# Encoder layer on one core: a planner that counts a transfer's packets, bias copies made in the prompt's attention, and two more buffers for reloaded rows

## The chip, the core and the metric

The kernel runs on one core of one Trainium2 chip. Its engines are TensorE (PE, the matmuls; PEld is its weight load), VectorE (DVE), ScalarE (ACT), GpSimd (POOL) and SyncE (SP), and here SP issues nearly all transfers of the 16 DMA engines. The metric is the device time of one execution in microseconds (us). Before the change it is 1153.21 us, the median of 3 runs (1151.79 to 1153.78).

## The reference

One layer of a bidirectional encoder is applied with the same weights to two inputs: a prompt of 512 tokens and a sample of 1024 tokens, each 1024 wide, all in float32.

```python
h = rmsnorm(x, norm_g)
proj = h @ w_in
qa, ka, va, za, qb, kb, vb, zb, ga, gb = jnp.split(proj, np.cumsum(SPLITS)[:-1], axis=-1)
qa = rmsnorm(qa.reshape(B, L, H_A, HEAD_DIM), qn_a)     # ka, qb, kb likewise
oa = neighbourhood_attention(qa, ka, va, rpb_a) * jax.nn.silu(za)
oa = oa @ w_o_a
ob = window_gqa_attention(qb, kb, vb, t5_table, sink_b) * jax.nn.silu(zb)
ob = ob @ w_o_b
merged = jax.nn.sigmoid(ga) * oa + jax.nn.sigmoid(gb) * ob
return x + merged @ w_out
```

Branch A has 8 heads of 64 that attend to a clamped window of 8 by 16 neighbours on a grid 64 wide, with a learned relative bias `rpb`. Branch B has 8 query heads on 2 key heads, a window of 128 tokens to each side, a T5 bias and a sink logit.

## The kernel before

**Products.** A float32 product is made of three matmuls: each operand is split into a high part (ACT, a copy to a shorter mantissa) and a low part (DVE or POOL, the difference), and high*high, low*high and high*low are added up in PSUM. In the rows this is a group of three: `x<-hh,whi`, `x<-hl,whi`, `x<-hh,wlo` on lines 1292, 1293 and 1294 (512 columns each), and `p<-whi,hh`, `p<-wlo,hh`, `p<-whi,hl` on line 762 (384 columns).

**Stages.** The work runs in four stages: the prompt's attention (to about 213 us), the prompt's dense phase (to about 412 us; beside it the sample's rows are normalised), the sample's attention (to about 780 us) and the sample's dense phase. In an attention stage PE makes the projections of q, k, v (L762), transposes the normalised q and k (L862, from the tile `qk`), makes scores (L934), transposes the exponentials `sb` (L1001, after ACT's exp on L980) and multiplies with v (L1038). The norm of q and k before L862 is a chain over three engines: ACT squares the projection (`sq`, L781), DVE sums (`ss`, L786), POOL turns the sum into a factor (`rs_v` L793, `rs_r` L800), and DVE multiplies (`qk`, L817). In a dense stage come the gate paths z, the products with w_o_a and w_o_b, the merge gates g, and the output product with w_out.

**Fill products.** Some dense products need only `hh` and `hl`, the normalised rows, and are made inside the attention stages to fill PE's gaps: `d<-hh,fh` and its two partners. Each result leaves PSUM through one tile `fc` with a single buffer (L1523) and is stored to DRAM as `g_d` or `p_d` (L1408). The next leave can write `fc` only when the store before has landed.

**Bias copies.** Branch A's bias is read by each head as long rows. `expand` (L413) copies the table in DRAM into `rpb_x`, 16 copies of 96 KB for the prompt and 16 for the sample; in the attention stage a bias tile is loaded from there (L683). The prompt's copies are made at the start, and the sample's copies from 211.72 us on, in the prompt's dense phase.

**u loads.** In the sample's dense phase the gated branch outputs u are kept in DRAM (`u_d`) and loaded again for the last products (L1577) through the two buffers of the tile `ot`; they are split into high and low parts as tiles `T`.

**Normalising the sample.** For the sample's norm factors eight tiles of the input are loaded in the prompt's attention (L458, `xt<-in_x_s_dram`), and ACT squares and sums them (L461, tile `junk`).

**The order.** All instructions are put in order ahead of time by a list planner, the class `Flow`. Each operation has a priority, a planned duration on each engine that may take it, its operands and its tiles. `Flow.run` keeps a clock: whenever an engine is free it takes, by priority, the operation whose inputs have arrived and whose tiles have a free buffer. A transfer costs SP an issue time, its bytes queue behind the transfers before (`dma_free`), and it counts as landed some time after. What comes out is one fixed sequence for each engine. On the chip each engine works through its sequence in order and waits by semaphores; a late input then holds up everything behind it on that engine. So a change of any planned cost can move instructions anywhere.

```python
return self.op((("sp", 470),), lambda e: emit(), prio, lag=nbytes / 360, **kw)
...
    dma_free = max(dma_free, now + ns + 650) + got.lag
    at(dma_free + 950, 2, got)
```

## Time and profile before

| what | value |
|---|---|
| median of 3 runs | 1153.21 us (1151.79 to 1153.78) |
| the profiled execution's own time | 1154.72 us |
| its span in the profile | 1152.9 us |
| PE busy | 1133.5 us, 6127 matmuls |
| DVE, ACT, POOL busy | 829.1, 640.8, 258.9 us |
| DMA | 174.65 MB, 151 GB/s over the span |
| TensorE clock granted, mean | 0.998 |

The profile is of one execution. Times in its rows run from the start of the span. A matmul's busy time is modelled; what counts for PE is the distance from one start to the next, which is 0.227 us for 512 columns and 0.173 us for 384 columns where nothing is late. In a row of a timeline the bracket tells how long the engine stood idle before it, and what ended that.

### The profile page before, as it was taken

Reading aid. Unit: us, or ns where it says so; the run is one execution under the profiler, and the core shown is the slowest. Engines: PE = TensorE matmul, PEld = TensorE weight load, DVE = VectorE, ACT = ScalarE, POOL = GpSimd, SP = SyncE. Lnnn points to the kernel's source line nnn. Section 1 sums busy time; section 2 is a strip of 40 time slices with the busy share of each in tenths; the row PEclk is TensorE's granted clock in tenths of the full one; section 3 lists DMA queues with packets and bytes.
Section 4 is the critical chain, followed back from the end, with each engine's and each line's share of the span. In section 5 each row is a group of like instructions: output and inputs, shape, how many; then the busy total and the mean of one; then the engine's idle time right before and its main releaser. Section 6 shows DMA issues by size and latency. Waiting matters only on the chain.

```text
span 1152.9 us, 18448 instructions
## 1 busy us (share of the span) xinstructions
PE 1133.5 (98%) x6127; PEld 981.4 (85%) x6127; DVE 829.1 (72%) x1831; ACT 640.8 (56%) x1468; POOL 258.9 (22%) x316
## 2 busy tenths in 40 slices
PE   8999999999998999999999999999999999999998
PEld 6989998888876899999999898887888888788887
DVE  6777787387775467676768788866787875497984
ACT  6767887534343246565668988775432444342320
POOL 4642422000010033333322122110122231032110
PEclk9999999999999999999999999999999999999999
DMA  7844534587786432121213223238777756564062
GB/s 270 284 138 119 187 105 126 158 246 240 242 277 196 151 124 65 28 83 26 65 38 103 61 47 102 56 102 263 254 191 200 240 188 186 204 228 128 28 219 92
DMA packets 141313, 174.65 MB, mean 151 GB/s; under 512 B 38569, under 2 KB 77937, under 8 KB 141218
## 3 DMA queue, kind: packets, MB, share of 16 engines
q1 hardware_dynamic: 141218, 173.48, 49.5%
q8 instruction: 48, 0.79, 0.3%
q14 instruction: 47, 0.39, 0.1%
HBM read 134.51 MB, written 43.63 MB: 155 GB/s over the span
## 4 chain that ended last, share of the span: by engine, by line
PE 84%; DMA 6%; DVE 4%; ACT 2%; POOL 1%; issue 1%; SPq 1%; ACTq 0%; DVEq 0%; POOLq 0%
PE p L762 23%; PE x L1294 8%; PE x L1293 8%; PE x L1292 8%; PE x L1001 5%; PE x L1038 5%; PE x L934 4%; PE d L1292 4%; PE d L1294 3%; PE d L1293 3%; PE p L1293 3%; PE p L1292 3%; PE p L1294 3%; PE x L862 2%; DMA t_d<-xt 1%
## 5 line engine op out<-in xcount | busy, mean ns | idle before, releaser
L762 PE MATMUL p<-whi,hh 128*128 128x384 f32 x384 | 133.1, 347 | 0.0
L762 PE MATMUL p<-whi,hl 128*128 128x384 f32 x384 | 131.9, 344 | 0.0
L762 PE MATMUL p<-wlo,hh 128*128 128x384 f32 x384 | 130.9, 341 | 0.0
L1012 DVE TENSOR_TENSOR pp<-x,pp 128x512 fp32r<-128x512 f32 (+1 forms) x136 | 82.8, 639 | 46.2 <-ACT pp L1007 45.8
L980 ACT ACTIVATE sb<-sb,mx 128x384 f32<-128x384 f32 (+1 forms) x192 | 107.4, 564 | 15.4 <-DVE mx L971 15.1
L762 PE MATMUL p<-whi,hb 128*128 128x384 f32 x384 | 106.7, 345 | 0.0
L1174 ACT ACTIVATE whi<-raw 128x512 fp32r<-128x512 f32 (+1 forms) x124 | 73.7, 606 | 55.8 <-PE x L1293 23.0
L1294 PE MATMUL x<-T,wlo 128*128 128x512 f32 x256 | 99.9, 390 | 0.3 <-DVE wlo L1179 0.2
L1293 PE MATMUL x<-T,whi 128*128 128x512 f32 x256 | 99.9, 390 | 0.2 <-DVE T L1179 0.2
L1292 PE MATMUL x<-T,whi 128*128 128x512 f32 x256 | 99.7, 390 | 0.0
L1292 PE MATMUL x<-hh,whi 128*128 128x512 f32 (+1 forms) x232 | 90.5, 390 | 3.0 <-ACT hh L1174 2.9
L1293 PE MATMUL x<-hl,whi 128*128 128x512 f32 (+1 forms) x232 | 90.8, 391 | 0.5 <-DVE hl L1179 0.5
L1294 PE MATMUL x<-hh,wlo 128*128 128x512 f32 (+1 forms) x232 | 90.5, 390 | 0.2 <-DVE wlo L1179 0.2
L800 POOL TENSOR_TENSOR rs_r<-rs_v,mhalf 128x4 f32<-128x4 f32 (+1 forms) x72 | 85.6, 1189 | 5.5
L1179 DVE TENSOR_TENSOR wlo<-raw,whi 128x512 fp32r<-128x512 f32 (+1 forms) x101 | 67.3, 676 | 26.0 <-ACT whi L1174 23.8
L793 POOL TENSOR_SCALAR rs_v<-ss 128x4 f32<-128x4 f32 (+1 forms) x72 | 22.2, 308 | 282.9 <-DVE ss L786 270.0
L1007 ACT ACTIVATE pp<-x 128x512 fp32r<-128x512 f32 (+1 forms) x136 | 70.8, 560 | 17.5 <-PE x L1001 16.6
L1038 PE MATMUL x<-pp,v 128*128 128x256 f32 (+1 forms) x368 | 77.3, 321 | 0.0
L1179 POOL TENSOR_TENSOR wlo<-raw,whi 128x512 fp32r<-128x512 f32 (+1 forms) x23 | 29.9, 1300 | 202.8 <-DMA raw<-in_w_g_dram 119.8
L762 PEld LDWEIGHTS p<-whi,hh 128*128 128x128 f32 x384 | 72.5, 189 | 1.3 <-issue 1.0
L762 PEld LDWEIGHTS p<-wlo,hh 128*128 128x128 f32 x384 | 72.6, 189 | 1.0 <-issue 0.7
L762 PEld LDWEIGHTS p<-whi,hl 128*128 128x128 f32 x384 | 72.5, 189 | 0.8 <-issue 0.5
(354 smaller groups left out, 2917.2 us busy)
## 6 DMA issues: line engine op xcount, KB each, us to landing
raw<-in_w_g_dram SPq DMA_DIRECT2D x84, 256.0 KB
w<-in_w_att_dram SPq DMA_DIRECT2D x46, 384.0 KB
ot<-o_d SPq DMA_DIRECT2D x36, 256.0 KB
g_d<-C SPq DMA_DIRECT2D x34, 256.0 KB
raw<-in_w_z_dram SPq DMA_DIRECT2D x32, 256.0 KB
raw<-in_w_out_dram SPq DMA_DIRECT2D x32, 256.0 KB
fr<-in_w_g_dram SPq DMA_DIRECT2D x28, 256.0 KB
C<-g_d SPq DMA_DIRECT2D x24, 256.0 KB
```

The lines of the kernel that those rows point to most:

```text
L762: pe.matmul(ps.t[:, :GW], part[u](k), mv.t[:, c], start=k == 0 and m == 0, stop=k == KC - 1 and m == 2,)
L800: lambda e: nc.gpsimd.tensor_tensor(r.t[:, :nn], rv.t[:, :nn], mhalf[:, :nn], op=ALU.pow),
L980: act.activation(sb.t[:, :width], sb.t[:, :width], AF.Exp, bias=mx.t[:, col(i)], scale=-1.0, accum_out=sm.t[:, col(i)],)
L1001: pe.transpose(pt.t[:, u * P : (u + 1) * P], sbs[i].t[:, c * P : (c + 1) * P], ident)
L1007: lambda e, pt=pt, pp=pp, nn=nn: act.activation(pp.t[:, 0, :nn], pt.t[:, :nn], AF.Copy),
L1012: lambda e, pt=pt, pp=pp, nn=nn: dve.tensor_tensor(pp.t[:, 1, :nn], pt.t[:, :nn], pp.t[:, 0, :nn].bitcast(F32), op=ALU.subtract),
L1038: pe.matmul(out(), v.t[:, vs], mv(), start=first, stop=last)
L1174: (("act", ACT_(n)),), lambda e: act.activation(hi(), src(), AF.Copy), prio,
L1179: lambda e: engines[e].tensor_tensor(lo(), src(), hi().bitcast(F32), op=ALU.subtract), prio,
L1292: pe.matmul(out, hi.t[:, cs], mh(), start=first and k == 0, stop=False, **more)
L1293: pe.matmul(out, hi.t[:, cs], ml(), start=False, stop=False, **more)
L1294: pe.matmul(out, lo.t[:, cs], mh(), start=False, stop=last and k == len(ws) - 1, **more)
```

## The change

Four things are edited. First, the planner's model of a transfer. Its time in the DMA queue was the bytes by 360 a nanosecond; now it is the number of packets (`nbytes / run`) times a cost of each packet (`9 + run / 26` ns), over 16 engines. The landing is counted 1050 ns behind the queue instead of 950. The time of issue on SP was 470 ns for all; now it is 430 ns by default and 470, 560, 570, 610, 640 or 690 ns for some kinds. For the common load of 256 KB with packets of 2048 bytes the planned time from the start of the issue to the landing goes from 2.80 to 2.83 us; for the load of 512 KB with packets of 512 bytes (L556) from 3.53 to 4.15 us; for one bias copy from 2.62 to 2.94 us.

Second, the 16 bias copies of the sample are planned in the prompt's attention, with priorities 9 to 16 and a start tied to that stage's progress (`f.begun`); before, they came with the dense phase's priorities 54 to 61, behind the last exponential.

Third, the second half of the u loads (`n` = 1) uses the two buffers of the tile `fr`, which the first half does not use, so that four loads can be under way.

Fourth, the planned duration of one kind of multiply (`gv`, with a strided operand) is 890 instead of that of 512 columns.

```diff
-    def dma(self, emit, nbytes, prio, **kw):
-        return self.op((("sp", 470),), lambda e: emit(), prio, lag=nbytes / 360, **kw)
+    def dma(self, emit, nbytes, prio, run=2048, issue=430, **kw):
+
+        lag = nbytes / run * (9 + run / 26) / 16
+        return self.op((("sp", issue),), lambda e: emit(), prio, lag=lag, **kw)
...
                         dma_free = max(dma_free, now + ns + 650) + got.lag
-                        at(dma_free + 950, 2, got)
+                        at(dma_free + 1050, 2, got)
...
-        f.dma(lambda: nc.sync.dma_start(xt.t, x[t * P : (t + 1) * P, :]), 524288, load_prio, new=[xt], after=load_after)
+        f.dma(lambda: nc.sync.dma_start(xt.t, x[t * P : (t + 1) * P, :]), 524288, load_prio, 4096, 470, new=[xt], after=load_after)
...
-                f.dma(lambda h=h, lo=lo: expand(geo, h, lo), 196608, prios[h], after=after[h // 2]) for lo in range(2)
+                f.dma(lambda h=h, lo=lo: expand(geo, h, lo), 196608, prios[h], 1536, 690, after=after[h // 2]) for lo in range(2)
...
-                tt(gv, gv, lambda: ov().rearrange("p (i n) -> p n i", n=m), ALU.mult, n, prio, use=[sg, ot], into=[sg])
+                tt(gv, gv, lambda: ov().rearrange("p (i n) -> p n i", n=m), ALU.mult, 890, prio, use=[sg, ot], into=[sg])
...
-                    st = tile_("ot", n_ot)
+                    st = f.value(wpool, [P, nh], F32, "fr", 2) if n else tile_("ot", n_ot)
...
+    expand_ops(gs, [9 + h for h in range(8)], [[f.begun[NT_P, 9 + 2 * i]] for i in range(4)])
...
-    expand_ops(gs, [4 + h for h in range(8)], [[exps]] * 4)
```

The other lines of the diff hand packet sizes and issue times to `dma`. Lines of the changed kernel behind L190 are two further down (L413 is L415, L1292 is L1294).

What the planner makes of it: PE's sequence is the same, product for product, from about 213 to 412 us and from about 802 us to the end, but for the products around 980 to 1009 us. It differs in both attention stages, up to about 802 us. DVE, ACT and SP have the same sequences from about 340 to 410 us and from about 1030 us on.

Place one is SP in the prompt's attention, at about 84 to 92 us of the profile before (`o_d` is a store of attention output, `line_d` a bias load of branch B, `in_w_att` a weight load, `in_x_s` a tile for the sample's norm). Before:

```order
L1062 DMA o_d_81<-ot__1254 64x2x128
L1066 DMA o_d_81<-ot__1265 64x2x64 x2
L601 DMA w_1337<-in_w_att_dram 128x768
L601 DMA w_1347<-in_w_att_dram 128x768
L458 DMA xt<-in_x_s_dram 128x1024
L601 DMA w_1435<-in_w_att_dram 128x768
```

And now:

```order
L711 DMA raw<-line_d 64x384
L415 DMA rpb_x_76<-in_rpb_dram 8x8x384
L1068 DMA o_d_81<-ot__1252 64x2x64 x2
L415 DMA rpb_x_76<-in_rpb_dram 8x8x384 x3
L603 DMA w_1331<-in_w_att_dram 128x768
L603 DMA w_1340<-in_w_att_dram 128x768
L460 DMA xt<-in_x_s_dram 128x1024
L603 DMA w_1418<-in_w_att_dram 128x768
L415 DMA rpb_x_76<-in_rpb_dram 8x8x384 x4
```

Three bias copies now stand directly ahead of two weight loads, and four stand behind the next one; four more are a little earlier and four later in this stage.

Place two is PE in the sample's attention, just ahead of the transposes at 448.22 us of the profile before (`ident,qk`). Before:

```order
L762 MATMUL p_5273<-whi_4713,hh_3168 128x384
L762 MATMUL p_5273<-wlo_4718,hh_3168 128x384
L762 MATMUL p_5273<-whi_4713,hl_3169 128x384
L762 MATMUL p_5273<-whi_4732,hh_3168 128x384
L762 MATMUL p_5273<-wlo_4739,hh_3168 128x384
L862 MATMUL x_5349<-ident_66,qk_5339 128x128 x2
```

And now:

```order
L764 MATMUL p_5266<-whi_4732,hh_3153 128x384
L764 MATMUL p_5266<-wlo_4739,hh_3153 128x384
L764 MATMUL p_5266<-whi_4732,hl_3154 128x384
L1294 MATMUL d_4933<-hh_3153,fh_4801 128x512
L1295 MATMUL d_4933<-hl_3154,fh_4801 128x512
L1296 MATMUL d_4933<-hh_3153,fl_4808 128x512
L1294 MATMUL d_4933<-hh_3153,fh_4801 128x512
L1295 MATMUL d_4933<-hl_3154,fh_4801 128x512
L1296 MATMUL d_4933<-hh_3153,fl_4808 128x512
L864 MATMUL x_5374<-ident_66,qk_5356 128x128 x2
```

Two fill products, six matmuls of 512 columns, stand ahead of the same transposes, and the rest of the projection has moved ahead of them too.

Place three is SP at the seam of the sample's attention and its dense phase, 781 to 794 us of the profile before (`U<-t_d` loads rows for the first dense products, `p_d<-fc` and `g_d<-fc` are the stores of fill products). Before:

```order
L1408 DMA g_d_96<-fc 128x512
L1511 DMA fr<-in_w_g_dram 128x512
L1423 DMA ot<-o_d_82 128x512 x2
L1244 DMA U<-t_d 128x512 x2
L1408 DMA p_d<-fc 128x512
L1244 DMA U<-t_d 128x512 x2
L1443 DMA fr<-n_d_80 64x512
L1256 DMA raw<-in_w_z_dram 128x512 x2
L1244 DMA U<-t_d 128x512 x2
L1408 DMA g_d_96<-fc 128x512
```

And now:

```order
L1410 DMA p_d<-fc 128x512
L1445 DMA fr<-n_d_80 64x512
L1425 DMA ot<-o_d_82 128x512 x2
L1246 DMA U<-t_d 128x512
L1445 DMA fr<-n_d_80 64x512
L1410 DMA g_d_96<-fc 128x512
L1246 DMA U<-t_d 128x512 x2
L1445 DMA fr<-n_d_80 64x512
L1246 DMA U<-t_d 128x512
L1258 DMA raw<-in_w_z_dram 128x512 x2
L1246 DMA U<-t_d 128x512
L1410 DMA p_d<-fc 128x512
```

The second store of this piece now has one U load ahead of it instead of two, and the fill group that is stored there has moved by one.

More of the change, by code (lines that the diff above doesn't have):

```diff
@@ L558, in norm_tile_t @@
             ),
-            524288, load_prio, new=[xt],
+            524288, load_prio, 512, 610, new=[xt],
         )
@@ L590, in norm_pair @@
                 ),
-                262144, prio, after=[o], hold=[(x0, x1)[dst[1]]],
+                262144, prio, 512, after=[o], hold=[(x0, x1)[dst[1]]],
             )
@@ L600, in att_weights @@
         sv = lambda: st.t[:, at : at + n]
-        ld = f.dma(lambda: nc.sync.dma_start(sv(), src), 512 * n, prio, after=after, **({"new": [st]} if new else {"hold": [st]}))
+        ld = f.dma(lambda: nc.sync.dma_start(sv(), src), 512 * n, prio, 3072, after=after, **({"new": [st]} if new else {"hold": [st]}))
         a = f.op(
@@ L683, in tables @@
                         lambda raw=raw, h=h: nc.sync.dma_start(raw.t[:, :run], rpb_x[nt][h]),
-                        run * 512, prio, new=[raw], after=expanded[nt, h],
+                        run * 512, prio, 4 * run, new=[raw], after=expanded[nt, h],
                     )
@@ L712, in tables @@
                         kw = {"new": [raw], "after": line_op} if lo == 0 else {"into": [raw]}
-                        sp(lambda raw=raw, h=h, lo=lo: emit_load(raw, h, lo), 98304, prio, **kw)
+                        sp(lambda raw=raw, h=h, lo=lo: emit_load(raw, h, lo), 98304, prio, 1536, 560, **kw)
                     def emit(e, i=i, raw=raw):
@@ L1066, in emit @@
                         nc.sync.dma_start(dst, ot.t[:64, 2 * i].rearrange("p (a b) -> p a b", b=64))
-                stores[g, runs[0][0] // 512].append(sp(emit, 65536, prio, use=[ot]))
+                stores[g, runs[0][0] // 512].append(sp(emit, 65536, prio, 512 // len(runs), 640 * len(runs), use=[ot]))
             else:
@@ L1074, in weigh @@
                         lambda e=e, dst=dst: nc.sync.dma_start(dst, ot.t[e * 64 : e * 64 + 64]),
-                        131072, prio, use=[ot],
+                        131072, prio, 512, 640, use=[ot],
                     )
@@ L1422, in post_z @@
                 dma(
-                    lambda dst=dst, src=src: nc.sync.dma_start(dst(), src), 512 * n, prio - 0.5, new=[ot],
-                    after=o_stores[c, a // nh],
+                    lambda dst=dst, src=src: nc.sync.dma_start(dst(), src), 512 * n, prio - 0.5,
+                    *((2048,) if c < 4 else (4 * m, 570)), new=[ot], after=o_stores[c, a // nh],
                 )
```

## The prediction

> **What bounds the kernel now.** I read the page's list of engines first, then the waits of PE, then the windows of 28.8 us, then the timeline at each place where a window is short.
>
> ```profile
> PE 1133.5 (98%) x6127; PEld 981.4 (85%) x6127; DVE 829.1 (72%) x1831; ACT 640.8 (56%) x1468; POOL 258.9 (22%) x316
> ```
>
> PE is busy for 1133.5 us of a span of 1152.9. The edits add no product and remove none, so only the other 19.4 us, and matmuls at a low clock, can be won. PE's waits say who held it up (us in total, times, longest):
>
> ```profile
> PE x L1669 <- DMA rb<-in_norm_row_dram: 4.7, 1, 4.7
> PE x L862 <- DVE qk L817: 3.2, 7, 0.6
> PE x L1292 <- ACT hh L1174: 2.9, 1, 2.9
> PE d L1292 <- ACT fc L1523: 1.7, 2, 1.4
> PE x L1001 <- ACT sb L980: 1.3, 4, 0.7
> ```
>
> The windows place them (start:end, length, then for each engine busy time and instructions; clock, DMA share, GB/s):
>
> ```profile
> 57.60:86.40 28.80, 26.96 (x173) 24.06 (x171) 20.14 (x56) 19.82 (x55) 13.76 (x24) 1.00 0.43 139
> 345.60:374.40 28.80, 25.27 (x102) 19.72 (x101) 16.78 (x27) 10.49 (x19) 1.60 (x2) 0.94 0.65 195
> 374.40:403.20 28.80, 28.80 (x129) 23.86 (x128) 12.06 (x16) 7.69 (x11) 0.00 (x0) 1.00 0.49 154
> 432.00:460.80 28.80, 28.25 (x191) 26.63 (x190) 20.34 (x58) 18.95 (x49) 9.65 (x11) 1.00 0.24 65
> 777.60:806.40 28.80, 27.11 (x120) 21.68 (x118) 17.30 (x28) 16.70 (x30) 0.00 (x0) 1.00 0.83 256
> 979.20:1008.00 28.80, 28.46 (x122) 22.41 (x121) 13.34 (x19) 10.10 (x17) 2.55 (x2) 1.00 0.62 211
> ```
>
> A window with nothing late has 129 matmuls. The one from 345.6 us has 102: 27 times 0.227 us is 6.1 us, the largest loss after the start. Its place:
>
> ```profile
> 363.10 0.49 PE L1292 MATMUL x<-hh,whi 128*128 128x512 f32 x1 [2.93 <-ACT hh L1174]
> 364.42 0.63 PE L1294 MATMUL x<-hh,wlo 128*128 128x512 f32 x1
> 364.85 0.63 PE L1292 MATMUL x<-hh,whi 128*128 128x512 f32 x1
> ```
>
> PE stood idle for 2.93 us, and then started matmuls 0.43 us apart instead of 0.227 (the window's clock is 0.94). This place, the start (4.7 us) and the tail lie where the sequences are unchanged, so I leave them as they are. What can change is the rest: some 4.5 us of waits in the two attention stages, some 2 us from 786 to 794 us, 1.4 us near 983 us.
>
> **Part by part.** *The planner's cost of a transfer, at the seam (term A).* A fill result leaves through the one buffer `fc`:
>
> ```profile
> 785.76 0.90 SPq L1244 DMA_DIRECT2D U<-t_d  x2
> 786.80 0.60 ACT L1523 ACTIVATE fc<-d 128x512 f32<-128x512 f32 x1 [3.97 <-DMA g_d<-fc]
> 787.42 0.32 SPq L1408 DMA_DIRECT2D p_d<-fc  x1
> 791.56 1.26 ACT L1174 ACTIVATE T<-U 128x512 fp32r<-128x512 f32 x2 [1.21 <-DMA U<-t_d]
> 793.25 0.58 ACT L1523 ACTIVATE fc<-d 128x512 f32<-128x512 f32 x1
> 793.87 0.50 PE L1292 MATMUL d<-hh,fh 128*128 128x512 f32 x1 [1.36 <-ACT fc L1523]
> ```
>
> The next leave stands on ACT behind two splits `T<-U` that wait for a U load, and its store was issued behind two such loads. From 787.42 to 793.25 us is 5.83 us, and PE started its next product at 793.87, 1.52 us late by its pitch. With 0.49 us at the leave before and some 0.2 at the restarts it lost 2.2 us here:
> ```profile
> 787.45 0.50 PE L1292 MATMUL d<-hh,fh 128*128 128x512 f32 x1 [0.33 <-ACT fc L1523]
> ```
>
> In the changed order one U load instead of two stands ahead of the second store, one split instead of two ahead of ACT's leave, and another leave goes to DVE. By pitches PE has 5.50, 6.42, 5.44 and 6.80 us of work from leave to leave, where it had 7.35, 5.44, 6.12 and 7.48. A cycle is a leave (0.60), an issue (0.32) and a landing of about 4 us (ACT's idle 3.97 before 786.80 was one store's landing), so 4.9 to 5.9 us with a wait on SP, and most of it fits: −1.6 us, between −2.2 and 0.
>
> *The norm chains (term B).*
>
> ```profile
> 442.89 0.39 ACT L781 ACTIVATE sq<-p 128x256 f32<-128x256 f32 x1
> 443.90 0.41 DVE L786 TENSOR_REDUCE ss<-sq 128x4 f32<-128x256 f32 x1
> 445.84 1.78 POOL L800 TENSOR_TENSOR rs_r<-rs_v,mhalf 128x4 f32<-128x4 f32 x1
> 447.65 0.42 DVE L817 TENSOR_TENSOR qk<-p,rs_r 128x256 f32<-128x256 f32 x1 [0.90 <-POOL rs_r L800]
> 448.22 0.41 PE L862 MATMUL x<-ident,qk 128*128 128x128 f32 x2 [0.55 <-DVE qk L817]
> ```
>
> From the last product of the projection (442.6) to the transposes the chain takes 5.6 us, and PE had 4.9 us of work. Now two fill products (six times 0.227, 1.4 us), four more projection matmuls (0.7) and three groups of `sb` transposes (some 0.5 each) stand between as well: 8.6 us. That wait goes, −0.7 us; its twin at 554.59 goes the same way, −0.7, and the one at 62.95 us has 6.3 instead of 5.5 us, −0.7:
>
> ```profile
> 62.95 0.41 PE L862 MATMUL x<-ident,qk 128*128 128x128 f32 x2 [0.56 <-DVE qk L817]
> 554.59 0.41 PE L862 MATMUL x<-ident,qk 128*128 128x128 f32 x2 [0.57 <-DVE qk L817]
> ```
>
> Against them: at 440.7 us the distance falls from 4.85 to 3.1 us, while the chain's own durations (0.39, 0.41, 1.78, 0.42, two gaps) are 3.2 to 3.8: +0.4. The twin at 500.7 us keeps its distance and its 0.7 us.
>
> *A fill product moved forward* near 626 us now stands directly behind the one whose result must first leave PSUM through ACT (0.58 us a leave); two groups of transposes stood between: +0.5 us. In the prompt's attention the wait for `sb` at 70 to 72 us (1.3 us with its restarts) has a score group of 0.9 us moved ahead of it: −0.7, between −1.3 and 0. What holds ACT there stays:
>
> ```profile
> 61.93 0.38 SPq L458 DMA_DIRECT2D xt<-in_x_s_dram  x1
> 68.96 1.06 ACT L461 ACTIVATE junk<-xt 128x1024 bf16<-128x1024 f32 x1 [2.17 <-DMA xt<-in_x_s_dram]
> ```
>
> The planner counts 3.5 us for this load, before and now; the chip took up to 7.0.
>
> *The bias copies.* Their issue costs SP 3.51 us for five, 0.7 each:
>
> ```profile
> 211.72 3.51 SPq L413 DMA_DIRECT2D rpb_x<-in_rpb_dram  x5
> 89.61 1.38 SPq L601 DMA_DIRECT2D w<-in_w_att_dram  x2
> 92.80 0.85 ACT L603 ACTIVATE whi<-w 128x768 fp32r<-128x768 f32 x1 [1.15 <-DMA w<-in_w_att_dram]
> 95.42 0.49 ACT L980 ACTIVATE sb<-sb,mx 128x256 f32<-128x256 f32 x1
> 96.25 0.60 PE L1001 MATMUL x<-ident,sb 128*128 128x128 f32 x4
> ```
>
> They leave 211 to 235 us, where PE loses nothing: gain 0. Where they go SP is mostly idle, and DMA has a share of 0.43 at 139 GB/s (window from 57.6), so 323 GB/s when full. Three copies stand ahead of the weight loads of 89.61 us. They read and write 0.59 MB, 1.8 us at that rate, and their issue (2.1 us) falls into SP's idle time from 87.9 us on. The load, which landed 3.2 us after issue, then lands up to 1.8 us later, at 94.6; ACT's exp waits behind `whi`. As the second `whi` (0.85 us and a wait of 0.53) has moved behind the exps, 1.4 us of that is taken up: +0.4 us, between 0 and +1.
>
> *Four buffers for u (term D).*
>
> ```profile
> ACT T L1174 <- DMA ot<-u_d: 18.9, 12, 2.8
> 979.01 0.37 SPq L1577 DMA_DIRECT2D ot<-u_d  x1
> 983.27 0.50 PE L1293 MATMUL x<-T,whi 128*128 128x512 f32 x1 [0.23 <-DVE T L1179]
> 984.33 0.63 ACT L1174 ACTIVATE T<-ot 128x512 fp32r<-128x512 f32 x1 [1.84 <-DMA ot<-u_d]
> ```
>
> Twelve splits waited 18.9 us for loads that two buffers let out too late; the load issued at 979.01 was used at 984.33, 5.3 us later, where the planner counts 2.8. Little of it reached PE: 1.4 us near 983 us with the restarts. With four buffers the third and fourth load go out with the first two, long before, and the later ones up to two loads earlier: −0.7 us, between −1.4 and +0.8 (splits moved from POOL to DVE, and a new product order). The longer cost of `gv` only moves order; no PE row waits on it: 0.
>
> The Trainium skill speaks against the constant landing ("DMA: Bandwidth & Descriptors", section "Latency and other measured facts"): HBM's access takes 0.2 us on average and 2 us at high load, so a planner with one constant is late just where queues are full. This trace agrees with 5.3 us at 979 against 2.8 planned. By it term D would hang on the buffers alone.
>
> *What I can't see one by one.* Some 540 us of attention order are new, with waits of the same kind; the old order has 4.5 us of them. For new ones I take +1.0 us, between 0 and +2.5.
>
> The sum: −1.6 −1.4 −0.7 +0.4 +0.5 −0.7 +0.4 −0.7 +1.0 = −2.8 us. On the profiled execution (1154.72 us, span 1152.9) it gives 1151.9 us, and on the median, which lies 1.5 lower, 1150.4.
>
> **Rivals.**
>
> *The waits only move.* For the common load of 256 KB the new cost is 2.83 instead of 2.80 us, so the planner has learned nearly nothing about the late transfers above, and the re-planned stages keep their 4.5 us. For it: the distance of 3.1 us at 440.7, the load of 61.93 still counted at 3.5. Against: the twins of term B and the seam are met by name. With attention at 0 net, the seam and u at half (−1.4), and +0.9 for the copies and 626 us: −0.5, 1152.7 us.
>
> *Slower: the copies starve the weight load at 89.6 us.* If a copy holds the queue for longer than its bytes need (nothing in the trace waits for one, so its time is not seen), ACT stands at `whi` and the exps behind it, and PE runs dry at the transposes of 96.25 us. It decides from a landing about 5 us later than now (98 us instead of 92.8): PE then idles some 2.9 us and more, and by the place at 363 us such a gap costs 6.1 us with the low clock behind it. −2.8 +6.1 −0.4 is +2.9: 1156.1 us. Against it: 0.59 MB would have to take nearly three times its 1.8 us.
>
> The Trainium skill ("TensorE: Matmul & The Clock Gate", section "What's actually happening") lets the clock fall after an idle window of about 3.4 us that runs freely, so a gap of 2.9 need not cost the clock. In this trace one of 2.93 us did.
>
> *Much faster: the gap at 363 us closes too.* Its `hh` waits on loads and a DVE queue whose order is the same; only the DMA load before 290 us is lighter. −2.8 −6.1: 1144.3 us.
>
> **How the numbers follow.** Chances: my sum 0.52, waits only move 0.24, a starved load 0.17, the gap at 363 closes 0.07. About 0.2% (2.3 us) is what a measurement of this kernel can tell from no change. My sum lies 0.5 us beyond that bound, and its own range by the ends of the terms is about 1147 to 1153.2: 0.36 of its chance I give to faster, 0.15 to same, 0.01 to slower. The second case gives 0.05, 0.16 and 0.03, the third 0, 0.03 and 0.14, the fourth all to faster. Together: faster 0.48, same 0.34, slower 0.18. The range for 8 in 10 goes from 1147.0, the low end of the sum's own, to 1155.8, which takes in most of the third case.
>
> **What would show it.** Right: `PE d <- ACT fc` falls from 1.7 to under 0.6 us; `PE x <- DVE qk` falls from 3.2 to about 2; the wait of T for u loads falls far below 18.9 us and is named on `fr` too; the windows of 345.6 us still has about 102 matmuls. The copies' term shows as ACT's wait for `in_w_att` near 93 us. Wrong: a clock below 1.00 in a window other than the one of 345.6 us; a new row in PE's waits of over 2 us; or a total of attention waits over 5 us.

## The result

The change made the kernel faster: 1144.68 us, the median of 8 runs (1142.22 to 1150.16), where 8 runs of the kernel before, the three named above among them, had 1153.49 us (1151.36 to 1157.50). The ratio is 0.9925, with an interval from 0.9903 to 0.9948. The forecast was 1150.4 us with a range from 1147.0, so the direction was right and the gain about three times the forecast one. The profiled execution of the changed kernel has a span of 1141.8 us, 11.1 us less than the one before.

The list of engines on its page, and the waits of PE over the whole kernel (us in total, times, longest):

```profile
PE 1129.1 (99%) x6127; PEld 981.4 (86%) x6127; DVE 825.1 (72%) x1824; ACT 640.8 (56%) x1465; POOL 258.8 (23%) x326
```

```profile
PE x L1671 <- DMA rb<-in_norm_row_dram: 4.6, 1, 4.6
PE x L535 <- DVE xt L523: 1.2, 1, 1.2
PE x L864 <- DVE qk L819: 0.9, 2, 0.6
PE d L1294 <- ACT fc L1525: 0.9, 1, 0.9
```

The row `PE x<-ACT hh`, with its single wait of 2.9 us, is gone, and the chain through `qk` has fallen from 3.2 to 0.9 us. PE's busy time is 4.4 us smaller for the same 6127 matmuls, in part since the 3.4 us at half clock behind the gap are gone: behind the first 14 us no stretch of the changed kernel's span runs at a low clock. The windows that answer to those of the prediction:

```profile
57.60:86.40 28.80, 28.80 (x190) 27.14 (x188) 22.11 (x65) 20.85 (x56) 12.89 (x24) 1.00 0.52 155
345.60:374.40 28.80, 28.80 (x129) 23.85 (x128) 14.32 (x22) 9.07 (x15) 1.29 (x1) 1.00 0.62 183
432.00:460.80 28.80, 28.80 (x196) 27.51 (x195) 21.71 (x63) 20.45 (x57) 6.35 (x12) 1.00 0.24 65
777.60:806.40 28.80, 28.80 (x128) 23.84 (x127) 20.10 (x34) 15.70 (x27) 1.29 (x1) 1.00 1.00 316
979.20:1008.00 28.80, 28.53 (x124) 23.06 (x125) 19.80 (x30) 10.42 (x17) 7.36 (x5) 1.00 0.63 194
```

The window from 345.6 us, which I had left as it was at 102 matmuls, is full: 129, clock 1.00.

Both kernels have 6127 matmuls, so the n-th start of one can be set against the n-th start of the other. The table shows by how much the changed kernel's PE is earlier (minus) or later at the matmul that the kernel before started at the given time. It compares two executions, so single steps carry the chance of both; the last part comes back to how much that is.

| at (us of before) | 60 | 100 | 213 | 355 | 375 | 440 | 610 | 780 | 806 | 1010 | 1145 |
|---|---|---|---|---|---|---|---|---|---|---|---|
| after | +2.70 | −0.30 | +1.40 | −0.62 | −6.72 | −7.10 | −9.99 | −8.84 | −11.63 | −10.78 | −10.78 |

The largest step, 6.1 us, is the place at 363 us. Then come the prompt's attention from 60 to 100 us (3.0), the sample's attention from 440 to 610 us (2.9), and the seam (2.8). The start lost 2.7 us.

ACT at the place around 355 us. In the kernel before, with SP's load for it first:

```profile
353.40 0.33 SPq L1603 DMA_DIRECT2D ot<-g_d  x1
...
356.91 0.63 ACT L1401 ACTIVATE ot<-ot 128x512 f32<-128x512 f32 x1 [2.35 <-DMA ot<-g_d]
362.42 0.63 ACT L1174 ACTIVATE hh<-C 128x512 fp32r<-128x512 f32 x1 [2.80 <-DVE C L1168]
```

And in the changed kernel:

```profile
345.42 0.36 SPq L1605 DMA_DIRECT2D ot<-g_d  x1
...
348.23 0.63 ACT L1403 ACTIVATE ot<-ot 128x512 f32<-128x512 f32 x1 [1.66 <-DMA ot<-g_d]
355.85 0.63 ACT L1176 ACTIVATE hh<-C 128x512 fp32r<-128x512 f32 x1 [1.47 <-DVE C L1170]
359.18 0.63 ACT L1176 ACTIVATE whi<-raw 128x512 fp32r<-128x512 f32 x1 [2.08 <-PE x L1295]
```

Each engine has the same sequence here in both kernels, and yet the load left 8 us earlier and `hh` came 6.6 us earlier. In the last row ACT waits for PE: the engines that feed PE are ahead of it. In the kernel before ACT waits between 340 and 363 us for a DMA and for DVE, never for PE. Call PE's lead the work whose inputs are ready when a feeding engine falls behind. Then the place at 363 us looks like the one where PE's lead ran out, not the one where the time was lost; the experiments test that.

### The profile page after: what moved, and what is told of

It reads as the page before. It is cut to its first block, busy times and chain, and to the rows that moved or that the text cites. A ratio compares the mean times of both kernels' runs of the same rounds, so it can differ in the third digit from the quotient of the medians.

```text
span 1141.8 us, 18502 instructions
## 1 busy us (share of the span) xinstructions
PE 1129.1 (99%) x6127; PEld 981.4 (86%) x6127; DVE 825.1 (72%) x1824; ACT 640.8 (56%) x1465; POOL 258.8 (23%) x326
## 5 line engine op out<-in xcount | busy, mean ns | idle before, releaser
L1294 PE MATMUL x<-T,whi 128*128 128x512 f32 x256 | 99.7, 389 | 0.0
L1294 PE MATMUL x<-hh,whi 128*128 128x512 f32 (+1 forms) x232 | 89.8, 387 | 0.0
L802 POOL TENSOR_TENSOR rs_r<-rs_v,mhalf 128x4 f32<-128x4 f32 (+1 forms) x72 | 81.7, 1134 | 5.7
L764 PEld LDWEIGHTS p<-whi,hb 128*128 128x128 f32 x384 | 69.2, 188 | 2.9 <-issue 0.5
```

Of the source, the lines that this page charges most:

```text
L764: pe.matmul(ps.t[:, :GW], part[u](k), mv.t[:, c], start=k == 0 and m == 0, stop=k == KC - 1 and m == 2,)
L802: lambda e: nc.gpsimd.tensor_tensor(r.t[:, :nn], rv.t[:, :nn], mhalf[:, :nn], op=ALU.pow),
L1294: pe.matmul(out, hi.t[:, cs], mh(), start=first and k == 0, stop=False, **more)
```

## The experiments

My theory after the result (theory R in the expectations): the sample's bias copies, at their old place, held SP for 13.9 us (the issue rows of its 16 copies between 211 and 235 us, added up). SP works in order, so all loads behind them left late, the feeding engines (ACT, DVE, and SP with its loads) stayed late for 120 us, and PE paid when it had no lead left. The rival that I set against it (theory P): the new planner costs did it, by handing the prompt's dense phase over in a better state. A second one: not SP's time but the copies' bytes in the DMA queues were the cost.

### The copies alone, to a place where SP is free

The kernel before, all its sequences kept; the 16 copies are taken out of SP's sequence and put back between its issues at 365 to 388 us (`f.late` holds them, and `PUT_OFF` gives the index on SP behind which two each go out).

```diff
+PUT_OFF = {321: 2, 323: 2, 325: 2, 327: 2, 328: 2, 329: 2, 330: 2, 332: 2}
...
-f.dma(lambda h=h, lo=lo: expand(geo, h, lo), ...
+f.dma(lambda h=h, lo=lo: f.late.append(lambda: expand(geo, h, lo)) if geo.nt == NT_S else expand(geo, h, lo), ...
```

> Every engine's sequence as in the kernel before, but the sample's 16 bias copies are issued at about 370 to 395 us instead of 211 to 235 us. Theory R (relief): copies in the first 25 us of the prompt's dense phase delay the loads of that phase, and the lateness lasts to the gap at 363 us; without them the gap of 2.93 us is gone, the window from 345.6 us has 129 matmuls, and the time falls by 6 to 8 us, to 1145 to 1147.5. Theory P (re-plan): the gap closed in the changed kernel because SP's loads between 213 and 340 us stand in another order; then the gap stays here and the time is that of before, 1152.5 to 1154.

Measured: 1148.46 us (7 runs) against 1154.87 us, ratio 0.9947 (0.9926 to 0.9967). That is −6.4 us from moving 16 transfers and nothing else. The window at the gap is full:

```profile
345.60:374.40 28.80, 28.80 (x129) 23.85 (x128) 15.41 (x24) 8.99 (x16) 1.29 (x1) 1.00 0.71 208
```

SP's rows at the old place, in the kernel before, behind the row of five copies that the prediction shows, and the six `fr` loads that stand behind them all:

```profile
217.82 2.75 SPq L413 DMA_DIRECT2D rpb_x<-in_rpb_dram  x4
...
223.29 3.69 SPq L413 DMA_DIRECT2D rpb_x<-in_rpb_dram  x1
...
227.52 2.01 SPq L413 DMA_DIRECT2D rpb_x<-in_rpb_dram  x3
...
235.16 3.70 SPq L1443 DMA_DIRECT2D fr<-n_d  x6
```

And in the experiment, the same six `fr` loads, and SP and ACT ahead of the place at 363 us:

```profile
227.91 4.17 SPq L1443 DMA_DIRECT2D fr<-n_d  x6
...
347.01 0.33 SPq L1603 DMA_DIRECT2D ot<-g_d  x1
...
355.86 0.63 ACT L1174 ACTIVATE hh<-C 128x512 fp32r<-128x512 f32 x1 [2.06 <-DVE C L1168]
361.33 0.63 ACT L1174 ACTIVATE whi<-raw 128x512 fp32r<-128x512 f32 x1 [2.09 <-PE x L1293]
```

Since the sequences are the same, every instruction can be matched. The median shift of this kernel against the one before, by stretch (us):

| stretch | 205–211 | 228–236 | 250–270 | 290–310 | 330–345 | 345–356 | 365–372 |
|---|---|---|---|---|---|---|---|
| SP | +0.9 | −6.9 | −4.9 | −5.0 | −5.8 | −6.4 | −6.4 |
| ACT | +0.9 | −3.2 | −4.4 | −5.0 | −5.9 | −6.6 | −7.3 |
| DVE | +0.9 | −3.2 | −4.4 | −5.0 | −5.8 | −6.4 | −6.8 |
| PE | +0.9 | +0.9 | +0.9 | −0.2 | −1.2 | −1.2 | −7.3 |

SP gains 7.8 us within 25 us, ACT and DVE follow, and through the next 120 us all three stay some 4 to 7 us ahead of the kernel before. PE moves by 2.1 us in this time, for it has work from its lead, until the place at 363 us. That is the mechanism. Some of the gain is given back at once, at the first norm chain of the sample's attention, which PE now reaches early:

```profile
406.83 0.44 PE L862 MATMUL x<-ident,qk 128*128 128x128 f32 x2 [1.66 <-DVE qk L817]
```

### The changed kernel with the copies back at the old place

The same device, on the changed kernel: all the new sequences, the copies at about 211 to 238 us.

```diff
+PUT_OFF = {175: 5, 179: 4, 185: 1, 186: 3, 187: 1, 191: 1, 198: 1}
```

> Every engine's sequence as in the changed kernel, but the sample's 16 bias copies are issued where the kernel before has them (behind the same stores and loads, from about 212 us on). Theory R: the gap near 358 us comes back, with the low clock, and the time rises by 6 to 8 us over the changed kernel, to 1151 to 1153. Theory P: as the changed kernel, 1144 to 1146.

Measured: 1151.5 us (12 runs), ratio 0.9966 (0.9946 to 0.9986), against 0.9925 for the changed kernel. The gap is back (the window, and PE's rows in it):

```profile
345.60:374.40 28.80, 24.06 (x92) 18.53 (x92) 17.73 (x29) 10.23 (x19) 2.58 (x2) 0.88 0.65 197
```

```profile
359.79 0.50 PE L1294 MATMUL x<-hh,whi 128*128 128x512 f32 x1 [1.51 <-ACT hh L1176]
...
364.26 0.79 PE L1294 MATMUL x<-hh,whi 128*128 128x512 f32 x1 [2.93 <-ACT hh L1176]
```

So the new order doesn't close the gap while the copies stand at the old place. The first rival falls as the explanation of this place. It stands for the rest: with the copies back, the kernel is still 3.4 us faster than before.

The mean granted clock of each run says the same without a trace, since 3.4 us at half clock lower it by 0.0015. It was 1.000 in 14 of 76 runs of the kernel before, in 4 of 7 with the copies late, in 13 of 14 of the changed kernel and in 0 of 12 with the copies back. So a fall of the clock belongs to most executions of the kernel before, though not to all.

### SP's time or the bytes

As in the first experiment the real copies go out late, and at each old place now stands a dummy copy with as many rows, of 16 bytes instead of 1536.

```diff
+src = bass.AP(tensor=rpb.tensor, offset=off, ap=[[16, geo.cw], [2, geo.rh], [1, cut or run]])   # cut = 4 floats
+f.dma(lambda h=h, lo=lo: (f.late.append(lambda: expand(geo, h, lo)), expand(geo, h, lo, 4)) if geo.nt == NT_S ...
```

> As the run with the copies issued late, but at the old places from 211 us on SP also issues 16 transfers with the same pattern and rows of 16 bytes instead of 1536, so that SP's time is spent as before and nearly no bytes move. If SP's time is what delays the dense phase, the gap at 363 us is back and the time is that of before, 1153 to 1155. If it is the copies' bytes in the DMA queue, the gap stays away and the time is that of the late copies, 1147 to 1149.

Measured: 1156.15 us (12 runs) against 1153.75, ratio 1.0007 (0.9989 to 1.0024): the whole gain of the first experiment is gone again. SP's rows of the dummies:

```profile
214.47 3.51 SPq L413 DMA_DIRECT2D rpb_y<-in_rpb_dram  x5
...
220.58 2.77 SPq L413 DMA_DIRECT2D rpb_y<-in_rpb_dram  x4
...
225.93 2.80 SPq L413 DMA_DIRECT2D rpb_y<-in_rpb_dram  x1
```

Their issue takes as long as that of the real ones (3.51 us for five in both, 2.77 for four against 2.75), though they move about a hundredth of the bytes. They have as many packets as the real ones, but the packets weren't in the way either: the DMA engines had a mean busy share of 0.40 over the row of five, and for its last 2 us they moved next to nothing (at most 6 GB/s), while SP went on issuing. So it is SP's time that costs. This profiled execution lost its time in two places instead of one: at the old place a shorter wait, at full clock, and then one at the sample's first norm chain, which it reached with the feeders still late:

```profile
364.20 0.50 PE L1292 MATMUL x<-hh,whi 128*128 128x512 f32 x1 [1.76 <-ACT hh L1174]
...
414.18 0.69 PE L862 MATMUL x<-ident,qk 128*128 128x128 f32 x2 [2.09 <-DVE qk L817]
```

Against the kernel before it lost 3.5 us at the second with the low clock behind it. Of its 12 runs one had a mean clock of 1.000. Late feeders present the bill at whichever place PE's lead runs out.

### The copies on another engine's queue

The kernel before, with the sample's copies issued from ACT instead of SP.

```diff
-nc.sync.dma_start(dst, src)
+(nc.scalar if geo.nt == NT_S else nc.sync).dma_start(dst, src)
```

> The kernel before, with the sample's 16 bias copies issued at the same places of the program from ACT instead of SP: the same bytes move from about 211 us on, but SP's 10 us are free. If SP's time is the cause, the dense phase runs as with the late copies and the gap at 363 us goes: 1147 to 1149. If the bytes are, the gap stays: 1153 to 1155.

Measured: 1157.21 us (12 runs) against 1155.37, ratio 1.0015 (0.9998 to 1.0031): no gain, and the gap is there as in the kernel before (at 366.50 us). Its row of PE's waits, then ACT's rows:

```profile
PE x L1292 <- ACT hh L1174: 2.9, 1, 2.9
```

```profile
216.74 4.69 ACTq L413 DMA_DIRECT2D rpb_x<-in_rpb_dram  x3
221.47 1.28 ACT L1401 ACT_TABLE_LOAD   x1 [4.88 <-DMA rpb_x<-in_rpb_dram]
...
229.68 0.60 ACT L1401 ACTIVATE C<-p 128x512 f32<-128x512 f32 x1 [5.80 <-DMA rpb_x<-in_rpb_dram]
```

By the expectation that outcome speaks for the bytes. But ACT feeds PE too, and it now stands idle for 4.9 and 5.8 us around the copies. Each issue took 0.65 us on ACT; the first row holds a stretch of 2.7 us between two issues, in which ACT's sequencer did not go on, and what held it isn't shown. By 290 us all feeders were 3.6 us later than in the kernel before. So I had not foreseen what the issue costs ACT, and this run can't tell bytes from issue; that rests on the dummies alone.

### The parts alone

**The planner's costs** (first edit) on the kernel before, copies at the old place.

> The kernel before with the first edit alone: the planner's new cost of a transfer, all else as before. Theory R: the gap at 363 us stays; the waits in the sample's attention and at the seam near 790 us may go, 1148.5 to 1153. Theory P: the gap closes too, 1144 to 1147.

Measured: 1150.82 us (12 runs) against 1154.87, ratio 0.9959 (0.9939 to 0.9980). In its trace the seam's window is full and the gap is smaller. But the profiled execution took 1146.48 us, the second fastest of the 12, and is one of three with a mean clock of 1.000; the other nine lie at 0.999 or below. So a typical execution of this kernel has more of the gap than the trace shows:

```profile
345.60:374.40 28.80, 27.07 (x119) 21.85 (x118) 17.82 (x28) 10.55 (x19) 1.30 (x1) 1.00 0.71 219
777.60:806.40 28.80, 28.80 (x129) 23.76 (x128) 17.52 (x29) 15.20 (x26) 1.29 (x1) 1.00 0.91 288
```

```profile
359.69 0.51 PE L1294 MATMUL x<-hh,whi 128*128 128x512 f32 x1 [1.50 <-ACT hh L1176]
```

By the n-th matmul this execution gains 2.8 us at the seam (780 to 806 us), as the changed kernel does, and 2.9 us from 440 to 610 us.

**The move** (second edit) on the kernel before.

```diff
+    expand_ops(gs, [9 + h for h in range(8)], [[f.begun[NT_P, 9 + 2 * i]] for i in range(4)])
-    expand_ops(gs, [4 + h for h in range(8)], [[exps]] * 4)
```

> The kernel before with the second edit alone: the bias copies are planned in the prompt's attention, the planner's costs are the old ones. Theory R: the gap at 363 us closes, 1144 to 1149, the spread being what the re-planned attention does. Theory P: the gap stays, 1151 to 1155.

Measured: 1154.81 us (12 runs) against 1154.87, ratio 1.0003 (0.9987 to 1.0018). The window from 345.6 us is full here too, a gain of 6.1 us by the n-th matmul; it was spent in the prompt's attention, where with the old costs four copies stand ahead of the weight loads:

```profile
88.11 2.80 SPq L413 DMA_DIRECT2D rpb_x<-in_rpb_dram  x4
91.02 0.86 SPq L601 DMA_DIRECT2D w<-in_w_att_dram  x2
96.11 0.85 ACT L603 ACTIVATE whi<-w 128x768 fp32r<-128x768 f32 x1 [4.28 <-DMA w<-in_w_att_dram]
97.50 0.33 PE L1001 MATMUL x<-ident,sb 128*128 128x128 f32 x1 [0.93 <-ACT sb L980]
98.73 0.72 PE L1001 MATMUL x<-ident,sb 128*128 128x128 f32 x3 [0.90 <-ACT sb L980]
```

The load lands 5.1 us behind its issue, ACT stands 4.28 us, PE waits twice for `sb` and runs at half clock from 98.97 until 102.38 us. This is the mechanism of my rival of the starved weight load, with less price than I gave it: 3.2 us from 60 to 100 us, and 1.7 more by 213 us. The time is the one that theory P gave, but not for its reason: the gap did close.

**The move, with the four copies behind the weight loads.** To see whether that is all, the same kernel with these copies behind two weight loads and an input load (again by an index on SP).

> The run with the second edit alone, but four of the bias copies stand behind two weight loads and an input load instead of ahead of them (about 88 to 92 us); all other sequences are the same. If the copies starve the weight load there, ACT's wait of 4.28 us for it falls to about 1 us, the low clock near 100 us goes, and the time falls by 4 to 6 us to 1149 to 1151. If the gap there has another cause, it stays at 1154 to 1156.

Measured: 1150.76 us (12 runs) against 1153.75, ratio 0.9968 (0.9954 to 0.9982). The window from 86.4 us, of the move alone and then of this kernel:

```profile
86.40:115.20 28.80, 26.96 (x169) 25.19 (x170) 17.77 (x52) 18.68 (x50) 7.75 (x13) 0.94 0.45 130
```

```profile
86.40:115.20 28.80, 28.50 (x187) 26.57 (x186) 19.66 (x58) 21.47 (x56) 8.40 (x13) 1.00 0.48 144
```

Four issues a few us later win 4 us, and 12 of 12 runs have a mean clock of 1.000. From 100 to 213 us this execution still loses 2.5 us, with PE's order unchanged, so the other copies have a price too. The move pays where its copies don't stand ahead of a load that is due.

**Four buffers for u** (third edit) on the kernel before.

```diff
-st = tile_("ot", n_ot)
+st = f.value(wpool, [P, nh], F32, "fr", 2) if n else tile_("ot", n_ot)
```

> The kernel before with the third edit alone: four buffers for the u loads. All sequences are those of before up to about 905 us. Theory D (the prediction's term): the splits' wait for u loads shrinks and PE's 1.4 us near 983 us go, 0.7 to 1.4 us faster than before. Rival: the loads come earlier, but the new order of the products makes PE wait for the splits' low parts on DVE instead, 0 to +1 us.

Measured: 1154.8 us (12 runs) against 1153.75, ratio 1.0007 (0.9991 to 1.0023): nothing. ACT's waits from 905 to 1030 us in this kernel:

```profile
ACT T L1174 <- DMA fr<-u_d: 4.1, 3, 2.6
ACT T L1174 <- DMA ot<-u_d: 3.0, 5, 1.1
```

The waits fell from 18.9 to 7.1 us, as planned, and PE gained nothing from it: from 806 to 1010 us it lost 0.7 us against the kernel before.

### Where else the changed kernel can gain

**Old costs in the start.** PE had lost 2.7 us by 60 us in the changed kernel. Here the changed kernel's planner uses the old costs until its clock reaches 36 us.

```diff
+SWITCH = 36000
-ns = dict(o.choice)[e]
+ns = o.alt[0] if o.lag and now >= SWITCH else dict(o.choice)[e]
```

> The changed kernel, but the planner uses the old costs of a transfer for its first 36 us of planned time. If the loss of 2.2 us up to 30 us comes from the order that the new costs give there (bias loads between the weight loads), PE is back at the times of before at 30 us and the kernel gains up to 2.2 us on the changed one, 1142 to 1144, less what the re-planned rest does. If that loss is only of the one execution profiled, nothing changes there: 1144 to 1146.

Measured: 1142.42 us (6 runs) against 1153.75, ratio 0.9894 (0.9870 to 0.9917). It is the time that I expected, but the first 30 us don't explain it: there this execution is 1.44 us behind the one before, and another execution of the changed kernel 1.27. What the edit does is wider than its name: with other costs for 36 us the planner orders PE anew from 10 to 213 us. At 213 us this kernel is at −0.06 us, and four executions with the changed kernel's order of PE are at +0.94 to +2.18.

**Old costs also from 880 us on, and two buffers for u**, on top of the last.

> The changed kernel with the planner's old costs for the first 36 us and again from 880 us of planned time on, and the u loads in two buffers as before. If the loss of 0.85 us between 900 and 1010 us comes from the new order there, this is 0.5 to 1 us faster than the run with old costs in the first 36 us alone, 1141 to 1142; else 1142 to 1143.

Measured: 1143.0 us (6 runs) against 1155.37, ratio 0.9889 (0.9868 to 0.9910): no gain over the last one that could be told. Its profiled execution has a new wait, with 0.43 us from start to start behind it (its lines are one further down than those of the changed kernel):

```profile
899.70 0.77 PE L1295 MATMUL p<-T,whi 128*128 128x512 f32 x1 [2.40 <-DVE C L1171]
900.27 0.63 PE L1296 MATMUL p<-T,whi 128*128 128x512 f32 x1
900.69 0.63 PE L1297 MATMUL p<-T,wlo 128*128 128x512 f32 x1
```

The changed kernel has the same wait at 902.45 us with 0.22 us, another execution of it had 1.06, and the run with late copies below, whose sequences are the same there, two of 1.23 and 1.08. By the n-th matmul the place cost 0.5, 1.5 and 2.8 us in these three and 4.2 us here; the kernel with the old costs in the start alone lost nothing there. So PE comes close to DVE there in most of these kernels, and a lead won earlier can be lost again at this place. I didn't test what holds DVE.

**The changed kernel again**, beside the last one and the next.

> The changed kernel once more, for comparison with the next two on the same chip: 1144 to 1146.

Measured: 1146.31 us (6 runs), ratio 0.9925 (0.9898 to 0.9952).

**The changed kernel with the copies at 365 to 390 us**, to see what they cost in the prompt's attention.

> The changed kernel's sequences, with the sample's bias copies issued at about 365 to 390 us instead of the prompt's attention. If the copies cost something in the attention (the wait of 1.98 us for the weight load near 93 us, 0.8 us on PE), this is 0.5 to 1 us faster than the changed kernel; if that wait is hidden or given back, the same; if copies so shortly before the sample's first bias loads make the first transposes there wait, up to 1.5 us slower.

Measured: 1147.22 us (6 runs), ratio 0.9927 (0.9904 to 0.9949): the same, but these intervals leave room for 2 to 3 us either way. By the n-th matmul, from 60 to 213 us, the two executions with the copies in the attention gained 1.3 and 0.5 us, and two without them there (this one and the one with the copies back) 2.4 and 2.3. So where the change puts them they seem to cost 1 to 2 us. The profiled execution here loses that again at 902 us.

The three measurements with the new costs in the start (0.9925 twice, 0.9927) lie above both with the old ones (0.9894, 0.9889): some 0.3%, or 4 us. Single intervals overlap, but the five fall into two groups by that edit. It changes PE's order up to 213 us, and in the traces these kernels are 1.0 to 2.6 us ahead there; where the rest of the 4 us comes from isn't shown. The kernel with the old costs in the start is faster than the changed one.

## Why the prediction was right or wrong

**What failed** is one step, and the others were small beside it: "They leave 211 to 235 us, where PE loses nothing: gain 0", and with it "This place, the start (4.7 us) and the tail lie where the sequences are unchanged, so I leave them as they are." I had the issue row of 3.51 us for five copies before me. I asked what PE loses where the copies stand, and not what stands behind them on SP. The first experiment shows what it measured: −6.4 us. In the trace PE gains 8.2 us from 213 to 375 us and gives 1.6 back at 407. That sequences are unchanged says nothing of times: the same instructions of SP, ACT and DVE ran 4 to 7 us earlier. The rival "the gap at 363 us closes too", at 1144.3 us, came true. I had given it 0.07, with the reason that only the DMA load before 290 us is lighter; the load of SP was what counted. Of the signs that I named, the window of 345.6 us "still has about 102 matmuls" is the one that failed for this reason. That the time comes within 0.4 us of that rival's is partly luck: outside the gap the profiled execution gained 4.7 us where I had 2.8, by larger gains and losses than my terms.

How far chance goes can be read from six executions that have PE's order of the kernel before throughout or up to 980 us (copies late, dummies, copies on ACT, the move alone and with four copies put behind, four buffers). Against the one profiled before they are 0.6 to 2.2 us later at 60 us, 1.4 on average, and move by −1.6 to +0.9 us at the seam, −0.6 on average. So that execution had a good start and a bad seam.

The other steps, with the changed kernel's shift between the times given:

- *The seam (A)*: −1.6 forecast, between −2.2 and 0; measured −2.6 to −2.8 in the seven executions that have the new order. No wait for `fc` is left there. Some 0.6 of it is the bad seam of the one execution before, so the order is worth about 2.2 us, the low end of my range. The direction and the reason were right; the size was short, for nearly all of the 2.2 us goes and not 1.6 of it.
- *Norm chains (B) and the fill product*: from 440 to 610 us −2.9 in all executions with the new order (−0.2 to 0 with the old one), where I had −1.4 and +0.4. The twins at 448 and 554 us went as forecast. The one at 500.7 us, which "keeps its distance and its 0.7 us", went as well, and +0.4 for 440.7 us doesn't show. The fill product behind the leave cost +0.8 from 610 to 640 us (forecast +0.5), with its row:

```profile
616.21 0.50 PE L1294 MATMUL d<-hh,fh 128*128 128x512 f32 x1 [0.87 <-ACT fc L1525]
```

  This is also why `PE d <- ACT fc` stayed at 0.9 us, when I had said it would fall under 0.6: the seam's wait is gone, and this one has come.

- *The prompt's attention*: from 60 to 100 us −3.0. The forecast has −0.7 at 62.95, −0.7 at 70 to 72 and +0.4 for the copies, −1.0 in all; a wait for `qk` at 86.23 us went too. But from 100 to 213 us 1.7 us came back, in no row of PE's waits above 0.2 us, and 2.7 had been lost by 60 us. As a whole the stretch to 213 us lost 1.4 us. Of the 2.7 us at 60 us about half is chance, by the 1.4 above: five executions with the new order of the start lie between +1.5 and +4.0 there, 2.8 on average. So the new order costs some 1.5 us in the start, and 1.3 to 2.1 us from 100 to 213 us, where the old one without the copies has 0. The term for "what I can't see" (+1.0, up to 2.5) was real, and much of it lay in the start, which I had left as it was: that "the sequences are unchanged" holds for the wait of 4.7 us, but PE's order differs from 10 us on.
- *The copies at the weight load*: I put its landing at 94.6 us at the latest and the cost at +0.4. ACT had it at 93.24, and one wait came of it:

```profile
86.22 2.10 SPq L415 DMA_DIRECT2D rpb_x<-in_rpb_dram  x3
88.42 0.86 SPq L603 DMA_DIRECT2D w<-in_w_att_dram  x2
93.24 0.84 ACT L605 ACTIVATE whi<-w 128x768 fp32r<-128x768 f32 x1 [1.98 <-DMA w<-in_w_att_dram]
94.63 0.55 PE L1003 MATMUL x<-ident,sb 128*128 128x128 f32 x3 [0.59 <-ACT sb L982]
```

  The load landed 4.8 us behind its issue instead of 3.2, so 1.6 us later, where I had worked out up to 1.8. This step held. Its price on PE is 0.6 to 1.1 us by the two executions with and the two without the copies there (60 to 100 us), at the upper end of my 0 to +1. That the starved-load rival is real, with four copies ahead instead of three, is shown by the move alone.
- *u loads (D)*: −0.7 forecast, nothing measured. The waits fell as I said they would, but PE had cover for them: from 970 to 1010 us the kernels with four buffers lose 0.3 to 1.1 us against the execution before, and those with two move by −0.4 to +0.5. From 806 to 1010 us the changed kernel lost 0.85, in its other profiled execution 1.9, most of it at the wait for `C` at 902 us, for which I had no term.
- *The rival "the waits only move"* is wrong: the costs alone give 0.9959. Its sum was wrong too: half of the seam and u is −1.15, not −1.4, so it should have said 1153.0 us.

How the gain divides: the copies alone give 0.9947, the costs alone 0.9959, the whole change 0.9925. The product of the two would be 0.9906; the measured 0.9925 lies 0.2% above it, about what these intervals leave open. Inside the changed kernel the place of the copies is worth 0.9925 against 0.9966 with them back, some 4.7 us, and all the rest 3.9 us. That the copies seem to win less here than alone fits with their price in the prompt's attention and with a gap that the new order alone makes smaller in some executions; how much of each, the runs don't settle.

I had said that 0.2% is about what a measurement can tell. Single runs of the kernel before go from 1149.55 to 1159.35 us, 0.85%. Only ratios of medians over many runs are as good as 0.2%.

## What to carry to other kernels

When PE has a gap, follow the feeding engines back in time to the place where they last lost time, not to the place of the gap: if the feeders there wait for transfers and for each other but never for PE, then their lateness is old, and unchanged sequences there promise nothing. Cost each transfer by the issue time on its queue's engine and by what stands behind it, also where PE is busy throughout: a lead of PE hides the loss and pays it later, at once and with a low clock. When transfers are moved off a busy stretch, look which due load they now stand ahead of; here three copies ahead of a weight load cost about 1 us, and four cost 4 of the 6.4 us that the move could win.

## What the runs showed of the hardware

**Issue time does not go by bytes.** A copy of 64 rows held SP for 0.63 to 0.76 us, with rows of 1536 bytes and with rows of 16 bytes alike, while a load of 256 KB in 128 rows (`ot<-g_d`) held it for 0.33. The Trainium skill ("DMA: Bandwidth & Descriptors", section "Issuing engines are not separate DMA queues") calls the sequencer's time for a DMA usually small relative to the DMA itself. Here the 13.9 us of SP's time were worth 6.4 us of the kernel's, and issuing from ACT won nothing.

**An issue can be held.** Single copies at the old place took 2.80 us (dummies) and 3.69 us (kernel before). This is not a property of the copies: both stand behind the two loads of 512 KB in packets of 512 bytes (L556), and with the copies late the load that stands there then is held for 2.26 us instead of some 0.34. So some 3 of the 13.9 us are not the copies' own. In these three stretches the DMA engines were full (shares of 0.93 to 1.03), but so they were in the kernel before when three copies followed at 0.65 us each (1.04 from 227.52 us); full engines alone don't hold an issue. What does wasn't tested.

**The clock falls after shorter gaps than I thought.** It fell to about half behind single waits of 2.93, 2.40 and 2.09 us, and behind two of 0.93 and 0.90 us that lay 1.2 us apart from start to start. It held behind 1.76, 1.66 and 1.50 us. The clock stayed at half for 3.41 us in five traces and for 6.83 in two (four buffers, copies back), and matmuls of 512 columns then started 0.43 us apart instead of 0.227. So 3.41 us cost some 1.6 us of work: 1.4 us in the kernel with the dummies (2.09 us of wait, 3.5 lost), 1.8 in the one with two buffers at 902 us (2.40 and 4.2). Of the 6.1 us at 363 us, 3.1 are the wait's, some 2 lie behind it, a wait of 0.23 us among them, and 0.9 are small waits ahead of it. The Trainium skill ("TensorE: Matmul & The Clock Gate", section "What's actually happening") puts the idle window at about 3.4 us, running freely. None of these waits was as long as that, and the clock fell behind each of them; on this measure a gap of 2 us has to be counted with the clock behind it.

**The start differs between executions.** At 60 us the changed kernel, the one with the copies back and the one with the costs alone, which have the same order of PE up to there, lie between +1.48 and +4.03 us, and the six executions with the order of the kernel before between +0.63 and +2.18. A term of 1 us that rests on one profile of the start is not to be relied on.
